# Sharing the first tile's high parts, squaring four chunks at a time, and moving the last square: a hybrid decoder layer on one core

## The chip, the cores and the metric

The kernel runs on one core of a Trainium2 chip. The core has a matrix engine (TensorE, PE in the profile), three engines for element-wise work (VectorE or DVE, ScalarE or ACT, GpSimd or POOL) and queues for transfers (the one on SyncE is SP). Each engine works through its own list of instructions in order and waits on semaphores for the others. The metric is device time of one execution in microseconds (us), the median over several runs; lower is better.

## The reference

One layer of a decoder trunk, for 1024 positions of width 1024, in float32:

```python
h = rmsnorm(x, norm1_w)
proj = h @ w_in                       # one projection for both mixers
qkv_a = silu(causal_dwconv(...))      # mixer A: gated DeltaNet, 4 heads of 128
o_a = gated_delta_rule(l2norm(qa) * 128 ** -0.5, l2norm(ka), va, g, beta)
o_a = rmsnorm(o_a, gdn_norm_w) * silu(z)
o_b = dilated_attention(qb, kb, vb)   # mixer B: 8 heads of 64, three windows
x = x + concatenate([o_a, o_b]) @ w_out
h = rmsnorm(x, norm2_w)
u = causal_dwconv(h @ w_up, ffn_conv_w)
x = x + (silu(gate) * up) @ w_down    # gate and up are the halves of u
return rmsnorm(x, final_norm_w)
```

`rmsnorm` divides by the root of the mean square over the features. In the gated delta rule every head carries a 128x128 state through the sequence, chunk by chunk, and `o_a` is normalized per position and head.

## The kernel before, in words

Activations are held with features on the 128 partitions and positions along the row, so `x` is eight tiles (`xt`) of 128x1024. Every large float32 product is done as three products of a faster type: each operand is split into a high part and the low rest (`xhi`, `xlo`, `whi`, `wlo`), and `mm3` adds hi*hi, hi*lo and lo*hi. Below, a product of 128x512 of this kind is called a dense product.

**The order of the work.** A planner (`Weave`) runs the parts of the layer as generators ("streams") with levels of urgency. It keeps an estimate of when each tile will be ready (`account`, with a fixed cost and a cost per element for each engine, by the size of the first tile named in the call) and steps the most urgent stream that is ready. The order in which it records the products is PE's order. The instructions of the other engines are put in order by a scheduler behind it, by their priority and its own estimates; `ua` and `uv` are ScalarE and VectorE with high priority, `ac` and `ve` the same engines without, and `after` makes one instruction stand behind another on its engine.

**The parts that the change touches.**

- *The first tiles.* Nine warm-up products (`warm`) run while the first transfers land. `split_x` makes the high part of a tile of `x` on ScalarE (scaled by `n1`, the weights of the first norm) and then the low part on VectorE. Tile 0 comes in two halves of 512 positions; PE begins when the first half's high part is there. `first` does the first six banks of products (keys of three heads); beside it `norms` sums the squares (`acc`) on PE with a vector `ones`, makes `rst` (one over the root) and transposes it into `rstdB`, and `gates` makes the decays. `kprep` then works on a head's keys `kT`: it turns them by token (`ktok`), squares them and multiplies keys by keys (PE `ps<-kT`).
- *The chains.* `chain(h)` carries the state of one head through eight chunks of 128 positions. A step is a string of small products and short operations that need each other: `ct,kT` on PE, `r` on VectorE, `r,um` on PE, `wke` on VectorE and `w` on ScalarE, `wke,ktok` on PE, and the new state `ct` on VectorE. The output of chunk c lands in `vtok`; its square with the sum over the row (`osq`, `ms`) is taken on ScalarE. After the last chunk the whole head is scaled by a power of `ms` on GpSimd, and `finish` transposes it. Four chains run interleaved with dense products, which fill the waits of one chain.
- *The end.* The last stage of the MLP's down-projection (`mlp_down`) treats the last four output tiles by halves of 256 positions. `last_product` adds a bank to the residual (`add_to`), and `complete` squares the result for the final norm. The last square (`apart`) isn't added to the others but summed on PE as a second operand (`more` in `mean_of`). Then come the power on GpSimd, two transposes (`turned`), eight scalings (`scale_out`) and the last transfers. Scalings of tiles that are ready earlier are put behind the addition of the last bank by `anchor=fourth`.

Of the kernel before, what the change touches and what calls it, by code (L numbers as in the profile page):

```python
# [7 lines left out]
F32 = mybir.dt.float32  # L8
F32R = mybir.dt.float32r
AF = mybir.ActivationFunctionType  # L10
OP = mybir.AluOpType
AX = mybir.AxisListType
# [3 lines left out]
P = 128  # L16
# [131 lines left out]
def hybrid_layer(tc, I, out):  # L148
    nc = tc.nc
    wv = Weave()  # L150
    ve = Engine(wv, nc.vector, "vector", 0.07, 0.00105)
    ac = Engine(wv, nc.scalar, "scalar", 0.12, 0.00085)

    uv = Engine(wv, nc.vector, "vector", 0.07, 0.00105, first=tc.high_priority)
    ua = Engine(wv, nc.scalar, "scalar", 0.12, 0.00085, first=tc.high_priority)
# [7 lines left out]
    sp = es.enter_context(tc.tile_pool(name="sp", bufs=1))  # L163
# [3 lines left out]
    def tile_(pool, shape, dt, name, tag, bufs):  # L167
        return wv.slot(pool.tile(list(shape), dt, name=name, tag=tag, bufs=bufs), tag, bufs)
# [3 lines left out]
    def A(name, tag, dt=F32, shape=(P, 1024)):  # L172
        if tag in TURNS:
            i = turns[tag] = turns.get(tag, -1) + 1
            tag = TURNS[tag][i % len(TURNS[tag])]
        return tile_(lp, shape, dt, name, tag, SLOTS[tag])
# [4 lines left out]
    def const(name, shape, src=None):  # L181
        t = cp.tile(list(shape), F32, name=name)
        if src is not None:
            sy.dma_start(t, src)
        return t
# [3 lines left out]
    def after(inst, anchor, reason="keeps a slot free until it is needed"):  # L189
        tc.add_manual_dep(inst.ins, anchor.ins.name, order, reason=reason)  # L190

    def mm(dst, lhs, rhs, us, start=True, stop=True, **kw):
        tc.stamp_issue_order_token(nc.tensor.matmul(dst, lhs, rhs, start=start, stop=stop, **kw).ins, TOKEN)  # L193
        wv.product(us, dst, lhs, rhs)
# [47 lines left out]
    n1 = const("n1", [P, KT])  # L242
# [6 lines left out]
    def rsqrt(dst, src, n):  # L249
        po_.tensor_tensor(dst, src, mhalf[:, :n], op=OP.pow)  # L250
# [14 lines left out]
    def bank(tag, name="ps"):  # L265
        return tile_(pp_, (P, 512), F32, name, tag, 2)

    def next_bank(tag, *tiles, slack=0.0):

        while max(wv.need(*tiles), wv.slot_free(tag, 2)) + slack > 1e-3:  # L270
            yield max(wv.need(*tiles), wv.slot_free(tag, 2)) + slack
        return bank(tag)

    def half(i):
        return slice(i * 512, i * 512 + 512)

    def v8(t):
        return t.rearrange("p (c t) -> p c t", c=NCH)
# [7 lines left out]

    def split_x(xt, k, sl):
        hi, lo = xs[k]
        inst = ua.activation(hi[:, sl], xt[:, sl], AF.Copy, scale=n1[:, k:k + 1])
        if k == 0:  # L290
            after(inst, his[0] if sl.start else whis[0], "in the order of arrival")
        if k == 1:
            after(inst, whis[1], "the weights come first")
        his[k:] = [inst]
        lo_of[0] = uv.scalar_tensor_tensor(lo[:, sl], xt[:, sl], n1[:, k:k + 1], hi[:, sl].bitcast(F32), op0=OP.mult,
                                           op1=OP.subtract)
# [19 lines left out]
    for k in range(KT):  # L316
        xt = A("xt", ("kT*", "dv*")[k % 2])
# [200 lines left out]
    def small(name, bufs=2):  # L518
        return tile_(sp, (P, NCH), F32, name, name, bufs)
# [316 lines left out]
    def chain_load(h, s):  # L836
        t = A("qat", "go" if s == 1 and h < 2 else "qa", shape=(P, 2, 512))
        sy.dma_start(t[:, 0, :], qpark[h][:, half(s)])
        sy.dma_start(t[:, 1, :], atpark[h][:, half(s)])
        return t  # L840
# [3 lines left out]
    def chain(h):  # L844

        for i in range(H):
            yield from wv.until(("m", i))
            yield from wv.until(("v", i))
        d = G[h]
        kT, ktok, vtok, yt, ge, rq, gq, ke = [d[n] for n in ("kT", "ktok", "vtok", "yt", "ge", "rq", "gq", "ke")]  # L850
        if not ct:
            ct.append(A("ct", "uy", shape=(P, 8, P)))
        sts = ct[0][:, 2 * h:2 * h + 2, :]
        qa = chain_load(h, 0)
        ps = bank(("asc", "ch")[h // 2])
        ms = small("ms", 4)
        tg = str(h)
        st = None
        for c in range(NCH):
            cs = slice(c * P, (c + 1) * P)  # L860
            if c == 2 and h < 2:
                qb = chain_load(h, 1)
            if c == 3 and h >= 2:
                yield from wv.until(("c", h - 2, 3))
                qb = chain_load(h, 1)
            if c == 4:
                qa = qb
            qT, at = [qa[:, i, (c % 4) * P:(c % 4 + 1) * P] for i in range(2)]
            if c == 0:
                r = vtok[:, cs]  # L870
                yield wv.need(ps, vtok, yt)
            else:
                yield wv.need(ps, st, slack=HOP)
                mm(ps[:, 0:P], kT[:, cs], st, 0.215)
                r = tile_(sp, [P, P], F32, "r", "r" + tg, 1)
                uv.scalar_tensor_tensor(r, ps[:, 0:P], ngam[:, c, h:h + 1], vtok[:, cs], op0=OP.mult, op1=OP.add)
                yield wv.need(r, slack=HOP)
            mm(ps[:, P:2 * P], yt[:, c, :], r, 0.215)
            w = tile_(sp, [P, P], F32, "w", "w" + tg, 1)
            if c < NCH - 1:  # L880
                wke = tile_(sp, [P, P], F32, "wke", "r" + tg, 1)
                uv.tensor_scalar(wke, ps[:, P:2 * P], ke[:, c:c + 1], None, op0=OP.mult)
            ua.activation(w, ps[:, P:2 * P], AF.Copy)
            if c < NCH - 1:
                yield wv.need(wke, slack=HOP)
                mm(ps[:, 2 * P:3 * P], ktok[:, cs], wke, 0.215)
                sn = sts[:, c % 2, :]
                if c == 0:
                    uv.tensor_copy(sn, ps[:, 2 * P:3 * P])
                else:  # L890
                    uv.scalar_tensor_tensor(sn, st, ge[:, c:c + 1], ps[:, 2 * P:3 * P], op0=OP.mult, op1=OP.add)
            yield wv.need(w, qa, slack=HOP)
            po = yield from next_bank("atr")
            if c:
                mm(po[:, P:2 * P], qT, st, 0.215)
            mm(po[:, :P], at, w, 0.215)

            ua.activation(vtok[:, cs], po[:, :P], AF.Copy, scale=rq[:, c:c + 1])
            if c:
                uv.scalar_tensor_tensor(vtok[:, cs], po[:, P:2 * P], gq[:, c:c + 1], vtok[:, cs], op0=OP.mult,  # L900
                                        op1=OP.add)
            if c < NCH - 1:
                st = sn
            osq = tile_(sp, [P, P], F32, "osq", "osq", 1)
            ua.activation(osq, vtok[:, cs], AF.Square, accum_out=ms[:, c:c + 1])
            wv.done.add(("c", h, c))

        ve.tensor_scalar(ms, ms, 1.0 / 128, EPS, op0=OP.mult, op1=OP.add)
        rsqrt(ms, ms, NCH)
        po_.tensor_tensor(v8(vtok), v8(vtok), ms[:, :, None].to_broadcast([P, NCH, P]), op=OP.mult)  # L910
        wv.add(1, finish(h, vtok))

    def finish(h, osb):
        for hh in range(2):
            pt = yield from next_bank("atr", osb)
            for c in range(4):
                i = 4 * hh + c
                tp(pt[:, c * P:(c + 1) * P], osb[:, i * P:(i + 1) * P])
            ot = tile_(sp, [P, 512], F32, "ot", "t2", 2)
            ac.activation(ot, pt, AF.Copy, scale=gw2)  # L920
            sy.dma_start(mixer[h][:, half(hh)], ot)
        wv.done.add(("o", h))
# [589 lines left out]
    def part(m, hh, sl):  # L1512
        return slice(512 * hh + sl.start, 512 * hh + sl.stop)
# [6 lines left out]
    def complete(m, hh, sl, apart=False):  # L1520

        sp_ = part(m, hh, sl)
        x = x1h[m][:, sp_]
        sq = tile_(sp, [P, 512], F32, "sq3", "t2", 2)
        ac.activation(sq[:, sl] if m else rstdB[:, sp_], x, AF.Square)
        if apart:
            return sq
        if m:
            ve.tensor_tensor(rstdB[:, sp_], rstdB[:, sp_], sq[:, sl], op=OP.add)

# [93 lines left out]
    for h in range(H):  # L1624
        wv.add(1, chain(h))
# [65 lines left out]
```

## Time and the profile before

| | us |
|---|---|
| median of 3 runs | 1201.8 |
| the three runs | 1199.36, 1201.80, 1201.89 |
| the profiled execution: its time | 1200.36 |
| its span in the profile | 1198.6 |
| PE busy in it | 1187.5 |
| VectorE, ScalarE, GpSimd busy | 915.1, 574.8, 89.8 |

The span runs from the first instruction to the last; 1.8 us of the execution's time lie outside it. In rows of the timeline the first two numbers are the start in the span and the duration, then come engine, line, operation and the tiles (written <- read); what stands in brackets is the idle time of that engine just before, and what ended it. Tile names are those of the program, without buffer numbers, and all operations of a helper have its line: L193 is `mm`, L197 `tp`, L142 and L144 the calls of the engines without and with high priority.

### The profile page before, as it was taken

How to read it: one execution, taken by the hardware profiler on the slowest of the kernel's cores; microseconds unless marked ns; L12 is line 12 of the kernel's file. 1: busy time of each engine (PE TensorE's matmuls, PEld its weight loads, DVE VectorE, ACT ScalarE, POOL GpSimd, SP SyncE). 2: the span in 40 equal slices, each digit the busy share in tenths (PEclk: the TensorE clock that was granted, in tenths of full speed). 3: DMA queues.
4: the chain of work that ended last, by engine and by line, in shares of the span. 5: the costliest groups of instructions: out<-in, count | busy, mean ns of one | idle time of the engine just before them, and what ended most of it. 6: DMA issues, size and time to landing. Idle time of an engine off the chain costs nothing.

```text
span 1198.6 us, 18324 instructions
## 1 busy us (share of the span) xinstructions
PE 1187.5 (99%) x7050; PEld 983.7 (82%) x7050; DVE 915.1 (76%) x1450; ACT 574.8 (48%) x1126; POOL 89.8 (7%) x100
## 2 busy tenths in 40 slices
PE   9999999999999999999999999999999999999997
PEld 7888888888777778888888888888888888888886
DVE  7683975665355566777989888989898889999875
ACT  7275345355454443655544544445445454434441
POOL 0212010214311120000000000000000000000000
PEclk9999999999999999999999999999999999999998
DMA  7435234436634204543213223131222398557414
GB/s 237 107 95 150 85 109 127 152 113 183 224 95 124 73 28 128 180 154 110 88 54 104 90 70 106 53 106 60 99 90 69 109 371 292 192 157 229 160 53 141
DMA packets 85798, 154.80 MB, mean 129 GB/s; under 512 B 21168, under 2 KB 36304, under 8 KB 85712
## 3 DMA queue, kind: packets, MB, share of 16 engines
q1 hardware_dynamic: 84848, 152.85, 39.1%
q8 instruction: 55, 0.90, 0.3%
q10 hardware_dynamic: 864, 0.79, 0.2%
q14 instruction: 31, 0.25, 0.1%
HBM read 117.68 MB, written 35.93 MB: 128 GB/s over the span
## 4 chain that ended last, share of the span: by engine, by line
PE 95%; DVE 2%; ACT 2%; issue 1%; DMA 0%; POOL 0%; POOLq 0%; DVEq 0%; SPq 0%; ACTq 0%
PE ps L193 45%; PE pa L193 20%; PE dw L193 17%; PE pc L193 10%; PE ps L197 3%; DVE kT L142 1%; ACT sm L144 0%; DMA xt<-in_xT 0%; DVE x1h L142 0%; ACT whi L142 0%; PE pd L193 0%; DVE zz L142 0%; ACT dec L142 0%; DVE xr L142 0%; DVE rstdB L142 0%
## 5 line engine op out<-in xcount | busy, mean ns | idle before, releaser
L193 PE MATMUL dw<-pr 128*128 128x512 f32 (+1 forms) x984 | 211.3, 376 | 0.0
L193 PEld LDWEIGHTS dw<-pr 128*128 128x128 f32 x984 | 176.7, 188 | 33.6
L193 PE MATMUL ps<-xhi,whi 128*128 128x512 f32 x384 | 157.7, 411 | 0.3 <-ACT xhi L144 0.3
L193 PE MATMUL ps<-xhi,wlo 128*128 128x512 f32 x384 | 150.3, 391 | 0.0
L193 PE MATMUL ps<-xlo,whi 128*128 128x512 f32 x384 | 148.4, 390 | 0.0
L193 PE MATMUL pa<-T,pair 128*128 128x512 f32 x528 | 127.0, 389 | 0.0
L193 PEld LDWEIGHTS pa<-T,pair 128*128 128x128 f32 x528 | 99.0, 188 | 20.6
L193 PEld LDWEIGHTS ps<-xhi,whi 128*128 128x128 f32 x384 | 72.5, 189 | 19.6 <-issue 5.6
L193 PEld LDWEIGHTS ps<-xhi,wlo 128*128 128x128 f32 x384 | 72.4, 188 | 15.7
L193 PEld LDWEIGHTS ps<-xlo,whi 128*128 128x128 f32 x384 | 72.3, 188 | 12.5
L142 ACT ACTIVATE u<-pa 128x512 f32<-128x512 f32 x44 | 26.3, 598 | 107.2 <-PE pa L193 107.2
L142 DVE SCALAR_TENSOR_TENSOR y<-xu,fcw,y 128x1023 f32<-128x1023 f32 (+1 forms) x44 | 56.4, 1281 | 22.1 <-ACT y L142 22.0
L142 ACT ACTIVATE whi<-wst 128x1024 fp32r<-128x1024 f32 x36 | 38.2, 1063 | 65.4 <-PE ps L193 54.3
L193 PE MATMUL pa<-B,A 128*128 128x512 f32 x264 | 63.4, 389 | 0.0
L193 PE MATMUL pa<-T,S 128*128 128x512 f32 x264 | 63.4, 389 | 0.0
L193 PE MATMUL pc<-B,pair 128*128 128x512 f32 x264 | 63.4, 389 | 0.0
L193 PE MATMUL pc<-T,S 128*128 128x512 f32 x264 | 63.4, 389 | 0.0
L142 DVE TENSOR_TENSOR wst<-wst 128x512 f32<-128x512 f32 x88 | 60.5, 688 | 0.9
L193 PE MATMUL ps<-B,pair 128*128 128x512 f32 x252 | 60.5, 389 | 0.0
L142 POOL TENSOR_TENSOR rs<-rs,mhalf 128x2 f32<-128x2 f32 (+2 forms) x4 | 4.7, 1187 | 738.4 <-DVE rs L144 738.4
L142 ACT ACTIVATE pr<-wd 128x1024 fp32r<-128x1024 f32 x33 | 34.9, 1058 | 49.5 <-PE dw L193 37.0
L144 ACT ACTIVATE sm<-sm,mx 128x128 f32<-128x128 f32 (+7 forms) x64 | 35.4, 556 | 48.2 <-DVE mx L144 48.2
(248 smaller groups left out, 2411.1 us busy)
## 6 DMA issues: line engine op xcount, KB each, us to landing
wst<-in_wu SPq DMA_DIRECT2D x44, 512.0 KB, 3.7
wd<-in_wd SPq DMA_DIRECT2D x44, 512.0 KB, 4.5
upark<-y SPq DMA_DIRECT2D x22, 512.0 KB, 3.6
wst<-in_wi SPq DMA_DIRECT2D x21, 512.0 KB, 3.8
r<-upark SPq DMA_DIRECT2D x11, 512.0 KB, 7.5
r<-upark SPq DMA_DIRECT2D x22, 256.0 KB, 7.5
wa<-in_wd SPq DMA_DIRECT2D x22, 256.0 KB, 3.3
wst<-in_wv SPq DMA_DIRECT2D x8, 512.0 KB, 3.7
```

What stands on the lines that cost most here:

```text
L142: return getattr(eng, op)(*a, **kw)
L144: return getattr(eng, op)(*a, **kw)
L193: tc.stamp_issue_order_token(nc.tensor.matmul(dst, lhs, rhs, start=start, stop=stop, **kw).ins, TOKEN)
L197: tc.stamp_issue_order_token(nc.tensor.transpose(dst, src, ident if idt is None else idt).ins, TOKEN)
```

## The change

Three edits. (1) In `split_x`, for tile 0 alone, the second 256 columns of each half's high part are made by VectorE (a multiplication by `n1`) and only the first 256 by ScalarE. (2) In `chain`, a square with its row sum after every chunk is replaced by one 128x512 square after every fourth chunk, without high priority, and a VectorE reduction that sums it into four columns of `ms`; the tile is now of the ring `t2`, which has two buffers and which other parts use too. (3) In `complete`, the last square is a VectorE multiplication instead of a ScalarE square.

```diff
     def split_x(xt, k, sl):
         hi, lo = xs[k]
-        inst = ua.activation(hi[:, sl], xt[:, sl], AF.Copy, scale=n1[:, k:k + 1])
+        if k == 0:
+            mid = sl.start + 256
+            ve.tensor_scalar(hi[:, mid:sl.stop], xt[:, mid:sl.stop], n1[:, k:k + 1], None, op0=OP.mult)
+            inst = ua.activation(hi[:, sl.start:mid], xt[:, sl.start:mid], AF.Copy, scale=n1[:, k:k + 1])
+        else:
+            inst = ua.activation(hi[:, sl], xt[:, sl], AF.Copy, scale=n1[:, k:k + 1])
...
-            osq = tile_(sp, [P, P], F32, "osq", "osq", 1)
-            ua.activation(osq, vtok[:, cs], AF.Square, accum_out=ms[:, c:c + 1])
+            if c % 4 == 3:
+                osq = tile_(sp, [P, 4, P], F32, "osq", "t2", 2)
+                hs = half(c // 4)
+                ac.activation(osq.rearrange("p c d -> p (c d)"), vtok[:, hs], AF.Square)
+                ve.tensor_reduce(out=ms[:, c - 3:c + 1], in_=osq, op=OP.add, axis=AX.X)
...
         sq = tile_(sp, [P, 512], F32, "sq3", "t2", 2)
+        if apart:
+            ve.tensor_tensor(sq[:, sl], x, x, op=OP.mult)
+            return sq
         ac.activation(sq[:, sl] if m else rstdB[:, sp_], x, AF.Square)
-        if apart:
-            return sq
```

Since the planner counts these operations, its order of the products changes too, though the products stay the same. The following is one piece of the difference on PE between the first dense products: `ps<-ones,acc` are the sums of the norm.

```order
 L193 MATMUL ps<-xlo,whi 128x512
 L193 MATMUL ps<-xhi,wlo 128x512
-L193 MATMUL ps<-xhi,whi 128x512
-L193 MATMUL ps<-xlo,whi 128x512
-L193 MATMUL ps<-xhi,wlo 128x512
+L193 MATMUL ps<-ones,acc 128x1 x2
 L193 MATMUL ps<-xhi,whi 128x512
```

The sums now come where three dense products stood: 99 of these stand ahead of the first sum, and 102 did before. The transposes of `rst`, further on, have 120 ahead of them instead of 126. From the turning of the first keys on, after 192 dense products, PE's order is as before until the chains.

On VectorE in the chains, this is the piece around the second half of the steps of heads 0 and 1, before (numbers tell the buffers apart; `ps_2444` and `ps_2434` are the banks of heads 1 and 0, `ct` with `ge_582` is the state of head 1, `wke_2830` belongs to head 0):

```order
L144 SCALAR_TENSOR_TENSOR r_2812<-ps_2454,ngam_246,vtok_2027 128x128
L144 SCALAR_TENSOR_TENSOR ct_2430<-ct_2430,ge_628,ps_2464 128x128
L144 SCALAR_TENSOR_TENSOR ct_2430<-ct_2430,ge_582,ps_2444 128x128
L144 SCALAR_TENSOR_TENSOR vtok_2411<-ps_2816,gq_2325,vtok_2411 128x128
L144 TENSOR_SCALAR wke_2830<-ps_2434,ke_672 128x128
```

And the same place after (the bank numbers are two higher):

```order
L144 SCALAR_TENSOR_TENSOR r_2792<-ps_2456,ngam_248,vtok_2029 128x128
L144 SCALAR_TENSOR_TENSOR ct_2432<-ct_2432,ge_630,ps_2466 128x128
L142 TENSOR_REDUCE ms_2457<-osq_2773 128x4
L144 SCALAR_TENSOR_TENSOR ct_2432<-ct_2432,ge_584,ps_2446 128x128
L144 SCALAR_TENSOR_TENSOR vtok_2413<-ps_2796,gq_2327,vtok_2413 128x128
L144 TENSOR_SCALAR wke_2808<-ps_2436,ke_674 128x128
```

The reduction of head 2's first four chunks now stands between the two states, ahead of `ct` of head 1 and of `wke` of head 0. The other operations keep their order.

On VectorE at the end of the program, before (`x1h<-x1h,dw` is the addition of a last bank, `x1h<-x1h,fw,ps` scalings of the output, `rs` the mean of the last squares):

```order
L142 SCALAR_TENSOR_TENSOR x1h<-x1h,fw,ps 128x256 x2
L142 TENSOR_TENSOR rstdB<-rstdB,sq_10777 128x256
L142 TENSOR_TENSOR x1h<-x1h,dw 128x256
L142 SCALAR_TENSOR_TENSOR x1h<-x1h,fw,ps 128x256 x2
L144 TENSOR_SCALAR rs_10811<-ps 128x2
L142 SCALAR_TENSOR_TENSOR x1h<-x1h,fw,ps 128x256 x8
```

And after:

```order
L142 SCALAR_TENSOR_TENSOR x1h<-x1h,fw,ps 128x256 x2
L142 TENSOR_TENSOR rstdB<-rstdB,sq_10739 128x256
L142 TENSOR_TENSOR x1h<-x1h,dw 128x256
L142 SCALAR_TENSOR_TENSOR x1h<-x1h,fw,ps 128x256 x2
L142 TENSOR_TENSOR sq_10762<-x1h 128x256
L144 TENSOR_SCALAR rs_10773<-ps 128x2
```

The last square, which was at the end of ScalarE's list, now stands on VectorE behind two scalings of the output and ahead of the mean.

## The prediction

> **What bounds the kernel now.** I read the page first (busy time, the chain that ended last, the groups), then PE's own waits, then the timeline at four places: the first product, the first keys, the four chains, the last microseconds.
>
> ```profile
> span 1198.6 us, 18324 instructions
> PE 1187.5 (99%) x7050; PEld 983.7 (82%) x7050; DVE 915.1 (76%) x1450; ACT 574.8 (48%) x1126; POOL 89.8 (7%) x100
> PE 95%; DVE 2%; ACT 2%; issue 1%; DMA 0%; POOL 0%; POOLq 0%; DVEq 0%; SPq 0%; ACTq 0%
> L142 DVE TENSOR_TENSOR wst<-wst 128x512 f32<-128x512 f32 x88 | 60.5, 688 | 0.9
> ```
>
> PE is busy for 1187.5 of 1198.6 us. The change adds and removes no matrix product, so it can act only through the some 11 us in which PE is idle, and through products that run slowly. This is PE's list of waits (engine, tile, line, releaser: total, times, longest):
>
> ```profile
> PE ps L193 <- ACT w L144: 0.5, 1, 0.5
> PE ps L193 <- DVE ct L144: 0.5, 1, 0.5
> PE ps L193 <- ACT xhi L144: 0.3, 1, 0.3
> PE ps L193 <- ACT sq L142: 0.3, 1, 0.3
> PE ps L193 <- ACT sq L144: 0.2, 1, 0.2
> ```
>
> Each of the five is one event, and each lies where the change has a hand: `xhi` at the start, `sq` of L144 at the first keys, `ct` and `w` in the chains, `sq` of L142 at the end. All five together are 1.8 us, 0.15% of the span. That is the size of this case.
>
> **The start: shared high parts.** The timeline around the first product:
>
> ```profile
> 4.47 0.85 PE L193 MATMUL warm<-warm 128*128 128x128 f32 x3
> 4.88 1.33 ACT L144 ACTIVATE xhi<-xt,n 128x512 fp32r<-128x512 f32 x2 [1.17 <-DMA xt<-in_xT]
> 5.64 1.41 DVE L144 SCALAR_TENSOR_TENSOR xlo<-xt,n,xhi 128x512 fp32r<-128x512 f32 x2 [1.34 <-ACT xhi L144]
> 5.66 0.79 PE L193 MATMUL ps<-xhi,whi 128*128 128x512 f32 x1 [0.34 <-ACT xhi L144]
> 6.25 0.63 PE L193 MATMUL ps<-xhi,wlo 128*128 128x512 f32 x1
> 6.67 0.63 PE L193 MATMUL ps<-xhi,whi 128*128 128x512 f32 x1
> 7.10 0.46 PE L193 MATMUL ps<-xhi,wlo 128*128 128x512 f32 x1
> ```
>
> ScalarE makes both 512-wide halves in 1.33 us, so the first takes about 0.66 us and ends at 5.54; PE starts 0.12 us later. Now ScalarE makes 256 columns. Its 128x256 squares at the end take 0.42 us (row below), so its half ends at 4.88 + 0.42 = 5.30. VectorE was idle for 1.34 us before 5.64 and makes the other 256 meanwhile; nearest row for it is again a 128x256 operation, 0.42 us. PE can start at 5.42, 0.24 us sooner; the warm-up products end at 5.32. What this is worth depends on the clock. Products here start 0.42 to 0.43 us apart up to 7.10, and 0.22 apart later (65.40 and 65.62 below). If the fast rate begins at a fixed time, 0.24 us more of slow running does 0.24/0.425 = 0.56 of a product, worth 0.56 x 0.22 = 0.13 us. If it begins after a fixed number of products, the whole 0.24 is gained. The Trainium skill, page "TensorE: Matmul & The Clock Gate", section "Part 1: The HAM clock gate", says that the warm-up budget is a stretch of time and not a number of matmuls: by that rule the gain is 0.13, without it 0.24. One trace can't show which holds. I take **-0.13 us**, with 0 and -0.24 as ends. The second half's high part now waits on VectorE behind `xlo` of the first half, some 6.4 instead of 6.2; nine products stand ahead of its first reader, so that is covered.
>
> **The first keys: an order that shifts.** The planner is told of the earlier start and puts the sums of the norm three dense products sooner on PE, and the first transposes of `rst` six sooner (126 dense products stood ahead of them, now 120). The rows:
>
> ```profile
> 39.39 1.64 POOL L142 TENSOR_TENSOR rst<-rst,mhalf 128x8 f32<-128x8 f32 x1 [33.98 <-DVE rst L142]
> 42.94 0.60 PE L197 MATMUL ps<-ident,rst 128*128 128x128 f32 x4
> 63.52 1.14 ACT L142 ACTIVATE kT<-xr,gcw 128x1024 f32<-128x1024 f32 x1
> 64.56 0.57 ACT L144 ACTIVATE ktok<-ps 128x512 f32<-128x512 f32 x1
> 65.40 0.39 PE L193 MATMUL ps<-wlo,xhi 128*128 128x512 f32 x1
> 65.62 0.39 PE L193 MATMUL ps<-whi,xlo 128*128 128x512 f32 x1
> 66.20 0.60 PE L193 MATMUL ps<-kT 128*128 128x128 f32 x3 [0.19 <-ACT sq L144]
> ```
>
> `rst` is ready at 41.03 and read at 42.94, a slack of 1.9 us. Sums three products (0.7 us) sooner and readers six products (1.3 us) sooner leave 1.3 us, so no new wait. Everything that hangs on the norm (scaling, convolution, key decays) then runs up to 1.3 us sooner against PE, whose products of the keys stay in place. At 66.20 PE is late: from 65.62 to 66.20 is 0.58 us where 0.22 is the step, because ScalarE turned to `ktok` at 64.56, straight behind other work. If that work is over 0.5 us or more sooner, the whole 0.36 goes. I take **-0.35 us**, with 0 as the other end.
>
> **The chains: squares four at a time.** Removed are 32 squares of 128x128 with their accumulator reads; added are eight squares of 128x512 on ScalarE and eight VectorE reductions.
>
> ```profile
> L144 ACT ACTIVATE osq<-vtok x32: 293/310/312, 248.0 to 304.6; 128x128 f32<-128x128 f32 x32
> L144 ACT ACTIVATION_READ_ACCUMULATOR osq<-vtok x32: 185/187/192, 248.3 to 304.8; 128x1 f32 x32
> 254.28 1.08 DVE L142 TENSOR_TENSOR aqkv<-ps,rstdB 128x512 f32<-128x512 f32 x1 [0.24 <-PE ps L193]
> 255.58 0.49 PE L193 MATMUL ps<-ct,kT 128*128 128x128 f32 x2 [0.45 <-DVE ct L144]
> 271.48 0.68 DVE L144 SCALAR_TENSOR_TENSOR ct<-ct,ge,ps 128x128 f32<-128x128 f32 x2
> 272.34 0.72 DVE L144 TENSOR_SCALAR wke<-ps,ke 128x128 f32<-128x128 f32 x2
> 272.48 0.37 ACT L144 ACTIVATE vtok<-ps,rq 128x128 f32<-128x128 f32 x1 [0.53 <-PE ps L193]
> 272.51 0.39 PE L193 MATMUL ps<-ct,kT 128*128 128x128 f32 x2
> 272.75 0.30 ACT L144 ACTIVATE osq<-vtok 128x128 f32<-128x128 f32 x1
> 273.04 0.43 ACT L144 ACTIVATE w<-ps 128x128 f32<-128x128 f32 x2
> 273.36 0.49 PE L193 MATMUL ps<-wke,ktok 128*128 128x128 f32 x2 [0.47 <-ACT w L144]
> ```
>
> ScalarE loses up to 32 x (0.31 + 0.19) = 16 us and gets back 8 x 0.66 (a 128x512 half of the start) = 5.3. PE had waited for those squares at one place only, 273.36: `w` could not start at 272.75 because `osq` stood ahead. Without it `w` starts 0.29 sooner. But at this very place the new order puts a reduction between the two `ct` on VectorE. No row shows a reduction; the nearest is the 128x512 tensor-tensor, 0.69 us (ends 0.34, one chunk's operation, and 1.08, `aqkv`). The second `ct` ran from 271.81 to 272.16, and PE used it at 272.51. Behind a reduction that starts at 271.74 it starts near 272.35, ends near 272.70, and PE's `ct,kT` comes at about 272.78, 0.27 late. `wke` follows two VectorE steps later, near 273.2, and PE's `wke,ktok` near 273.3: where it stood anyway. One wait takes the place of the other: **0 us**. The wait at 255.58 is `aqkv` ahead of `ct`; both stand as before, so it stays. In the new order the first two reductions have three dense products (0.7 us) behind them before their neighbours on VectorE are read, and the last five have dense products around them, so I cost them at nothing; where that cover fails each costs up to 0.6 us (0.69 less the some 0.08 by which the next VectorE operation starts before the end, as the rows of the end show). The last scaling of a head now waits for a reduction before its power on GpSimd; its transposes stand behind that by more than a microsecond in my count. Bounds for the stage: -0.9 (both waits go) and +3.
>
> **The end: last square on VectorE.**
>
> ```profile
> 1188.99 0.42 DVE L142 TENSOR_TENSOR x1h<-x1h,dw 128x256 f32<-128x256 f32 x1
> 1189.33 0.87 DVE L142 SCALAR_TENSOR_TENSOR x1h<-x1h,fw,ps 128x256 f32<-128x256 f32 x2
> 1189.51 0.42 ACT L142 ACTIVATE sq<-x1h 128x256 f32<-128x256 f32 x1 [1.15 <-DVE x1h L142]
> 1189.97 0.61 PE L193 MATMUL ps<-ones,sq 128*128 128x1 f32 x4 [0.29 <-ACT sq L142]
> ```
>
> Here nothing covers: sum, power, transposes, scaling and output all hang on this square. ScalarE started 0.1 us after the addition and PE followed at 1189.97. On VectorE the square could run from 1189.33, but the new order puts it behind the two scalings that only had to follow the addition. They hold VectorE to 1190.12 (the 1189.33 row starts 0.08 us before the end of the one ahead); a 128x256 square of 0.42 us ends at 1190.54, and with 0.1 to 0.16 us of hand-over PE starts near 1190.67. That is **+0.70 us**; were the square ahead of the scalings, it would be 1189.75 and -0.1.
>
> **The sum.** -0.13 - 0.35 + 0 + 0.70 = +0.22 us on the profiled execution's 1200.36 us: 1200.6. The three timed runs have their median at 1201.8 and reach from 1199.36 to 1201.89, so the profiled one lies inside them. On the median the forecast is 1202.0 us.
>
> **The rivals.** *Reductions stop the chains (slower).* Around 255 and 273 us few or no dense products stand between dependent steps, and the row at 255.58 shows what one long VectorE operation does there: 1.08 us of `aqkv`, 0.45 of wait. If five of the eight reductions cost PE their full 0.6 us, the stage gives +3.0 and the time is 1205.0. It decides from four such reductions on (2.4 us); against it speak the dense products around most. Chance 0.20. *ScalarE's freedom pays (faster).* Both chain waits go (0.45 + 0.47), the start gives 0.24, the keys 0.35, and the end gains 0.1 because the scalings are not ready when the square is: -1.6, so 1200.2. The order on VectorE speaks against the last part, `aqkv` against the first. Chance 0.12. *The split does not do what it says:* VectorE's half ends as late as ScalarE's whole did, the start gives 0, and the time is 1202.1. Chance 0.05. The forecast has 0.63.
>
> **The numbers.** A difference of 0.2% (2.4 us) is about what a measurement of this kernel can tell from none. Forecast and split rival (0.68) lie within it, but for 0.03 at each side that the spread of single runs may carry over. The slow rival gives 0.20 to slower; the fast one crosses the bound only with that spread too, 0.09 of its 0.12. Faster 0.12, same 0.65, slower 0.23. The range leaves out some 0.1 at each side: from 1199.2 (fast rival, a low median) to 1204.8 (nearly all of the slow one).
>
> **What would show it.** In the new profile: PE's first product near 5.4 and the fast rate still from about 7.1; no wait of PE at 66; a reduction of about 0.7 us ahead of `ct` and a wait for `ct` where that for `w` was; the last square behind two scalings and its sums 0.7 us later against the last `dw` product. The forecast is wrong if the chains' stretch grows by more than a microsecond, or if the last sums do not move.

## The result and the profile after

The changed kernel takes 1202.97 us (median of 12 runs, 1202.73 to 1205.33), the kernel before 1200.40 us (median of 12 runs, 1199.36 to 1201.89; the first three runs, on which the forecast stood, had been high ones). The ratio is 1.0024, with a 95% interval of 1.0016 to 1.0032. The change makes the kernel 2.6 us slower; the forecast was +0.2 us. The time lies inside the range, but two of the four terms of the sum were wrong, a third can't be seen in the time, and a wait that the prediction had ruled out is the largest part.

The profiled execution of the changed kernel took 1203.51 us. The head of its page, and then the list of PE's waits (engine, tile, line, releaser: total, times, longest), without four waits that are as before (`ones`, `rs`, `sm`, `rstdB`):

```profile
span 1201.7 us, 18306 instructions
PE 1187.2 (99%) x7050; PEld 982.6 (82%) x7050; DVE 919.4 (77%) x1461; ACT 568.3 (47%) x1069; POOL 90.7 (8%) x100
```

```profile
PE ps L197 <- POOL vtok L142: 1.2, 2, 1.0
PE ps L193 <- DVE sq L142: 0.9, 1, 0.9
PE ps L193 <- ACT xhi L144: 0.8, 1, 0.8
PE ps L193 <- ACT sq L144: 0.6, 1, 0.6
PE ps L193 <- DVE acc L142: 0.5, 1, 0.5
PE ps L193 <- DVE ct L144: 0.5, 1, 0.5
PE ps L193 <- ACT w L144: 0.4, 1, 0.4
```

PE is as busy as before (1187.2 against 1187.5 us); ScalarE has lost 6.5 us of work and VectorE gained 4.3, and neither shows in the span. The waits sum to 4.9 us where the five of before made 1.8. That the difference, 3.1 us, equals that of the two spans is tempting, but the traces of the experiments show that the waits for `xhi` and for `sq` of L144 differ as much between executions with the same order of instructions (0.2 to 1.0 us and 0.2 to 1.1 us). Two of the others are surely the change's own: `vtok` on GpSimd, which was no wait before, and `sq` on VectorE at the end.

The start, in the timeline of the changed kernel:

```profile
5.05 0.91 ACT L144 ACTIVATE xhi<-xt,n 128x256 fp32r<-128x256 f32 x2 [0.66 <-DMA xt<-in_xT]
5.61 0.50 PE L193 MATMUL ps<-xhi,whi 128*128 128x512 f32 x1 [0.81 <-ACT xhi L144]
5.95 0.39 PE L193 MATMUL ps<-xhi,wlo 128*128 128x512 f32 x1
6.18 0.39 PE L193 MATMUL ps<-xhi,whi 128*128 128x512 f32 x1
```

The two shares take 0.91 us on ScalarE instead of 1.33, but the transfer landed 0.17 us later than in the profile before, so the first product stands at 5.61 instead of 5.66. And here the products ran at the fast step (0.23 us) from the second on; in the profile before they had been at 0.43 up to 7.10. The first keys:

```profile
58.88 1.88 DVE L142 SCALAR_TENSOR_TENSOR kT<-xr,kT 128x1024 f32<-128x1024 f32 x1 [0.59 <-ACT xr L142]
60.68 0.16 DVE L142 COPY gel<-dec 128x8 f32<-128x8 f32 x1
67.06 1.16 PE L193 MATMUL ps<-kT 128*128 128x128 f32 x8 [0.57 <-ACT sq L144]
```

The wait that should have gone grew from 0.19 to 0.57. The chains' last two heads, on GpSimd, then on PE, with the operations of ScalarE and VectorE that make the last `ms`:

```profile
294.98 1.64 POOL L142 TENSOR_TENSOR ms<-ms,mhalf 128x8 f32<-128x8 f32 x1 [2.11 <-PE ps L193]
296.85 2.39 POOL L142 TENSOR_TENSOR wlo<-wst,whi 128x1024 fp32r<-128x1024 f32 x1 [0.23 <-ACT whi L142]
299.19 1.90 POOL L142 TENSOR_TENSOR vtok<-vtok,ms 128x1024 f32<-128x1024 f32 x1
...
311.80 2.40 POOL L142 TENSOR_TENSOR wlo<-wst,whi 128x1024 fp32r<-128x1024 f32 x1 [2.72 <-ACT whi L142]
314.16 1.64 POOL L142 TENSOR_TENSOR ms<-ms,mhalf 128x8 f32<-128x8 f32 x1
315.87 1.90 POOL L142 TENSOR_TENSOR vtok<-vtok,ms 128x1024 f32<-128x1024 f32 x1
301.15 1.09 PE L197 MATMUL ps<-ident,vtok 128*128 128x128 f32 x8 [0.25 <-POOL vtok L142]
317.82 1.10 PE L197 MATMUL ps<-ident,vtok 128*128 128x128 f32 x8 [0.96 <-POOL vtok L142]
309.49 0.63 ACT L142 ACTIVATE osq<-vtok 128x512 f32<-128x512 f32 x1 [0.42 <-DVE vtok L144]
310.15 0.69 DVE L142 TENSOR_REDUCE ms<-osq 128x4 f32<-128x512 f32 x1 [0.70 <-ACT osq L142]
310.78 1.13 DVE L142 TENSOR_TENSOR aqkv<-ps,rstdB 128x512 f32<-128x512 f32 x1
311.75 0.17 DVE L142 TENSOR_SCALAR ms<-ms 128x8 f32<-128x8 f32 x1
```

A head's scaling is a power (1.64 us) and a multiplication (1.90) on GpSimd. In the kernel before they followed each other for every head; these are its last two:

```profile
293.24 1.64 POOL L142 TENSOR_TENSOR ms<-ms,mhalf 128x8 f32<-128x8 f32 x1 [1.24 <-DVE ms L142]
294.95 1.90 POOL L142 TENSOR_TENSOR vtok<-vtok,ms 128x1024 f32<-128x1024 f32 x1
296.81 2.38 POOL L142 TENSOR_TENSOR wlo<-wst,whi 128x1024 fp32r<-128x1024 f32 x1
...
305.31 1.64 POOL L142 TENSOR_TENSOR ms<-ms,mhalf 128x8 f32<-128x8 f32 x1 [1.22 <-DVE ms L142]
307.02 1.90 POOL L142 TENSOR_TENSOR vtok<-vtok,ms 128x1024 f32<-128x1024 f32 x1
```

There the next `wlo` came at 310.17 only, and PE's transposes of the fourth head at 311.04, 2.1 us after its scaling had ended. Now a dense weight's low part (`wlo`, 2.4 us) stands between them for the third head and ahead of both for the fourth, where `ms` is ready at 311.92 only: square 0.63, reduction 0.69, and then `aqkv`, 1.13 us, ahead of the small scaling of `ms` on VectorE. PE waits for both heads. The end:

```profile
1191.23 0.42 DVE L142 TENSOR_TENSOR x1h<-x1h,dw 128x256 f32<-128x256 f32 x1
1191.57 0.86 DVE L142 SCALAR_TENSOR_TENSOR x1h<-x1h,fw,ps 128x256 f32<-128x256 f32 x2
1192.35 0.42 DVE L142 TENSOR_TENSOR sq<-x1h 128x256 f32<-128x256 f32 x1
1192.82 0.61 PE L193 MATMUL ps<-ones,sq 128*128 128x1 f32 x4 [0.90 <-DVE sq L142]
```

The sums start 1.59 us after the last addition, where it was 1189.97 - 1188.99 = 0.98: 0.61 us later, through the two scalings, as forecast.

### The profile page after: what moved, and what is told of

The parts are those of the page before. It is cut to its first block, busy times and chain, and to the rows that moved or that the text cites. A ratio compares the mean times of both kernels' runs of the same rounds, so it can differ in the third digit from the quotient of the medians.

```text
span 1201.7 us, 18306 instructions
## 1 busy us (share of the span) xinstructions
PE 1187.2 (99%) x7050; PEld 982.6 (82%) x7050; DVE 919.4 (77%) x1461; ACT 568.3 (47%) x1069; POOL 90.7 (8%) x100
## 4 chain that ended last, share of the span: by engine, by line
PE 71%; DVE 1%; issue 1%; ACT 0%; POOL 0%; POOLq 0%; DVEq 0%; ACTq 0%
PE ps L193 23%; PE pa L193 20%; PE dw L193 17%; PE pc L193 10%; PE ps L197 2%; DVE x1h L142 0%; PE pd L193 0%; DVE zz L142 0%; ACT sm L144 0%; DVE rstdB L142 0%; POOL rs L142 0%; DVE pt L144 0%; POOLq L1696 0%; DVE xr L142 0%; DVE sm L144 0%
## 5 line engine op out<-in xcount | busy, mean ns | idle before, releaser
L142 ACT ACTIVATE pr<-r 128x1024 fp32r<-128x1024 f32 (+1 forms) x44 | 36.5, 839 | 47.0 <-PE dw L193 29.8
L193 PEld LDWEIGHTS pa<-B,A 128*128 128x128 f32 x264 | 49.6, 188 | 10.3
```

The costliest lines, as they stand in the source:

```text
L142: return getattr(eng, op)(*a, **kw)
```

## Experiments

Each was timed in five rounds against the kernel before on the same chip (medians of before there: 1200.15, 1200.25 and 1200.24 us for the three groups). One such ratio is uncertain by 0.0009, about 1.1 us, so the smaller terms are read from the traces. For that the table after the third group cuts each execution at the same products. The edits are shown shortened; a remark behind `#` stands for lines that are left out.

### First group: the edits one by one

**First edit alone.**

```diff
-        inst = ua.activation(hi[:, sl], xt[:, sl], ...)
+        if k == 0:   # 256 columns on VectorE, 256 on ScalarE
```

> The kernel before with the first edit alone (high parts of tile 0 shared). Theory A (the planner's shift costs more than the earlier start gives): the first product comes 0.05 to 0.25 us sooner, but the sums of the norm, three dense products earlier in PE's order, wait about 0.5 us for acc, and the first products of keys by keys still wait about 0.6; together +0.2 to +0.9 us against before (ratio 1.0002 to 1.0008). Theory B (the prediction: -0.13 at the start, -0.35 at the first keys): -0.5 us. Theory C: the waits of the changed kernel at 33 and 67 us came from transfers that landed late in that one execution; then they are gone here and the time is within 0.2 us of before.

Measured: 1200.44 us, ratio 1.0007 (0.9998 to 1.0016). The first product came at 5.36, the wait at the first keys was 0.69 us. The interval reaches from -0.2 to +1.9 us, so theory B's -0.5 lies outside it; theories A and C can't be told apart by the time. The wait for `acc` was down to 0.08 us, but late transfers alone don't explain that of the changed kernel. With the sums where they stood before (eight traced executions, those below included) PE never waited for `acc`, which was ready 0.36 to 1.69 us ahead; with the sums three products sooner (five) it waited 0.08, 0, 0.25, 0.29 and 0.50 us. The shift takes the slack, and how late `acc` is differs from execution to execution. The forecast's -0.35 at the keys did not show.

**Second edit alone.**

```diff
-            ua.activation(osq, vtok[:, cs], AF.Square, accum_out=ms[:, c:c + 1])
+            if c % 4 == 3:   # one 128x512 square and a reduction
```

> The kernel before with the second edit alone (squares four chunks at a time). Theory A (GpSimd's order): the power and the scaling of the heads 2 and 3 stand behind a dense weight's 2.4 us low part, PE waits about 1 us at one pair of head transposes and 0.4 at another, and the time grows by 1.2 to 1.8 us. Theory B (the prediction: one wait takes the place of another, transposes covered): within 0.2 us of before. Theory C (the reductions stop the chains): +3 us, and the waits lie at ct, r or wke on VectorE, not at vtok on GpSimd.

Measured: 1202.01 us, ratio 1.0017 (1.0009 to 1.0026). PE's waits in the chains' stretch of the trace are those of the changed kernel's list: 1.2 us in two events for `vtok` on GpSimd, 0.5 for `ct` and 0.4 for `w`. The last two were 0.5 each before. The new wait is for `vtok` alone: theory A, and no sign of theory C.

At the place that the prediction worked out, the reduction stands at 273.18 between the two `ct`, and the next `ct,kT` on PE comes 0.41 us after the product ahead of it where it was 0.23. The wait for `w` did not go with the square of ScalarE: `w` now waits for `wke`, which stands behind the reduction.

```profile
274.73 0.47 ACT L144 ACTIVATE w<-ps 128x128 f32<-128x128 f32 x2 [0.40 <-DVE wke L144]
```

**Third edit alone.**

```diff
-        ac.activation(sq[:, sl] if m else rstdB[:, sp_], x, AF.Square)
         if apart:
+            ve.tensor_tensor(sq[:, sl], x, x, op=OP.mult)
             return sq
```

> The kernel before with the third edit alone (last square on VectorE). Theory A (the square stands behind two scalings on VectorE): the last sums come 0.6 to 0.7 us later after the last addition, and the time grows by the same 0.6 to 0.7 us. Rival: the end hangs on the output transfers, which queue behind the earlier scalings anyway; then it is within 0.2 us of before.

Measured: 1200.95 us, ratio 1.0013 (1.0004 to 1.0022). The sums start 1.59 us after the last addition, 0.61 later than before, and the last stretch in the table below is 100.30 us where it was 99.69: theory A.

**All three edits, last square first.**

```diff
-            ve.tensor_tensor(sq[:, sl], x, x, op=OP.mult)
+            added.append(ve.tensor_tensor(sq[:, sl], x, x, op=OP.mult))
-        scale_out(0, left, pl, range(6, 8), anchor=fourth)
+        scale_out(0, left, pl, range(6, 8), anchor=added[-1])
```

> The changed kernel with all three edits, but the last two scalings of the left half put behind the last square on VectorE instead of behind the addition, so that the square comes first. Theory A (order is the whole cost of the third edit): 0.6 to 0.8 us less than the changed kernel, so about 1.8 us over before, with the sums waiting for sq about 0.1 to 0.2 us. Rival (VectorE's square is slower than ScalarE's or is handed over later): the gain is under 0.3 us.

Measured: 1202.66 us, ratio 1.0023 (1.0013 to 1.0032); only 0.3 us under the changed kernel by the medians. The trace shows the last stretch at 99.53 instead of 100.19, so 0.66 us came back there; its middle stretch was 0.5 us longer, with one pause of PE for VectorE (`x`) at 502 us that no other execution has at that place. So the medians leave it open, and the trace speaks for the theory.

### Second group: what in each edit costs

**Squares four at a time for the first four chunks only.**

```diff
+            if c == 3:   # as in the change, for chunks 0 to 3
+            if c > 3:    # as before, one square with a row sum
```

> The kernel before with the second edit for the first four chunks only: chunks 4 to 7 keep their square with a row sum on ScalarE, so that ms is ready as early as before, and GpSimd's order is the order of before. Theory A (the cost of the second edit is the late ms and what GpSimd does meanwhile): no wait of PE for vtok, and within 0.3 us of before, 1.4 us under the second edit alone. Rival (the four-chunk squares and reductions cost by themselves, or the three dense products that the planner moves do): half of the 1.4 us or more stays.

Measured: 1200.58 us, ratio 1.0006 (0.9997 to 1.0014). No wait for `vtok`; 1.4 us under the second edit alone by the medians. In the trace the chains' stretch is 164.42 us, 0.4 over before: most of the cost went, not all. PE's list for that stretch has `ct` (0.5 us) and `w` (0.3) and no new wait, so what the rest hangs on stays open.

**Second edit with GpSimd's order mended.**

```diff
-            po_.tensor_tensor(lo, st, hi.bitcast(F32), op=OP.subtract)
+            inst = po_.tensor_tensor(lo, st, hi.bitcast(F32), op=OP.subtract)
+            if "scaled" in last:      # a head's multiplication by ms
+                after(inst, last["scaled"], "the heads go first")
```

> The second edit alone, and in addition each dense weight's low part on GpSimd put behind the last head's scaling that was recorded ahead of it. Nothing else moves: the orders on TensorE, VectorE and ScalarE are those of the second edit alone; on GpSimd two low parts of 2.4 us go behind the scalings of heads 2 and 3. Theory A (GpSimd's order is the cost, not the lateness of ms by itself): the two waits for vtok (1.2 us together, 1.5 us with the hand-over) go, and the time is 1.2 to 1.6 us under the second edit alone, within 0.4 us of before. Rival 1 (ms is late in any case): the longer wait stays at 0.5 us or more. Rival 2 (the dense products then wait for their late low part): a new wait for wlo of about 1 us.

Measured: 1200.40 us, ratio 1.0000 (0.9991 to 1.0009). GpSimd at the last two heads, and PE at the last:

```profile
293.24 1.64 POOL L142 TENSOR_TENSOR ms<-ms,mhalf 128x8 f32<-128x8 f32 x1 [2.12 <-ACT ot L142]
294.95 1.90 POOL L142 TENSOR_TENSOR vtok<-vtok,ms 128x1024 f32<-128x1024 f32 x1
296.81 2.39 POOL L142 TENSOR_TENSOR wlo<-wst,whi 128x1024 fp32r<-128x1024 f32 x1
...
310.92 1.64 POOL L142 TENSOR_TENSOR ms<-ms,mhalf 128x8 f32<-128x8 f32 x1 [4.07 <-DVE ms L142]
312.63 1.90 POOL L142 TENSOR_TENSOR vtok<-vtok,ms 128x1024 f32<-128x1024 f32 x1
314.49 2.40 POOL L142 TENSOR_TENSOR wlo<-wst,whi 128x1024 fp32r<-128x1024 f32 x1
314.59 1.09 PE L197 MATMUL ps<-ident,vtok 128*128 128x128 f32 x8
```

Nothing but GpSimd's order differs from the second edit alone, and the whole cost is gone: 1.6 us by the medians (of two chips), 1.5 in the chains' stretch of the trace. No product waits for its later low part. Theory A, and it prices the rest of the second edit: eight reductions of 0.69 us and eight squares cost nothing that the chains' stretch as a whole shows (163.91 us; before, 164.02). Rival 1 lives on in small: the fourth head's scaling ends at 314.53 and PE reads at 314.59. Counted from the same product (the 5500th from the end, in the table below), its power starts 6.6 us later than before and PE's transposes 4.5 us later, so the late `ms` alone uses up the 2.1 us that were to spare.

**Third edit alone, square first.** The edit is that of the first group's last kernel, on the kernel before.

```diff
+            added.append(ve.tensor_tensor(sq[:, sl], x, x, op=OP.mult))
```

> The kernel before with the third edit alone, the square put ahead of the last two scalings on VectorE. Theory (only the order cost anything): the last sums come 0.1 to 0.2 us sooner than before; the time is 0.7 to 0.9 us under the third edit alone and within 0.2 us of before, too little for a verdict against before. Rival: VectorE's square is later in any case, +0.3 us or more.

Measured: 1200.44 us, ratio 1.0002 (0.9993 to 1.0011). VectorE and PE at the end:

```profile
1188.77 0.42 DVE L142 TENSOR_TENSOR x1h<-x1h,dw 128x256 f32<-128x256 f32 x1
1189.23 0.42 DVE L142 TENSOR_TENSOR sq<-x1h 128x256 f32<-128x256 f32 x1
1189.57 0.86 DVE L142 SCALAR_TENSOR_TENSOR x1h<-x1h,fw,ps 128x256 f32<-128x256 f32 x2
1189.70 0.61 PE L193 MATMUL ps<-ones,sq 128*128 128x1 f32 x4 [0.24 <-DVE sq L142]
```

The sums start 0.93 us after the addition (before 0.98, with the edit as it was 1.59). The order is the whole cost of the third edit. On VectorE the square starts 0.04 us after its own addition ends (1189.19), on ScalarE it was 0.10 (1189.51 after 1189.41); moving it gains 0.05 us.

**First edit, the planner's account unchanged.**

```diff
+            wv.account("scalar", 0.12 + 0.00085 * 512, [hi[:, sl]], [xt[:, sl], n1[:, k:k + 1]], 0.28)
+            nc.vector.tensor_scalar(hi[:, mid:sl.stop], ...)
+                inst = nc.scalar.activation(hi[:, sl.start:mid], ...)
```

> The kernel before with the first edit alone, but the planner's account kept as it was for the whole square of ScalarE, so that the order of the products on TensorE is that of before; only the two engines' shares are new. Theory A (an earlier first product is worth nothing that lasts, since TensorE's slow products end at a time that differs from execution to execution by more than the gain, and the first keys hang on VectorE's gel): the sixtieth product anywhere from 15.4 to 16.1 us as in the runs of an undivided start, and the time within 0.3 us of before. Rival (the gain was real and the moved products gave it back): 0.3 to 0.5 us under before, and the first keys' wait is shorter than in the runs of before's start.

Measured: 1200.09 us, ratio 0.9999 (0.9990 to 1.0008). First product at 5.49, sixtieth at 15.73 us, and a wait of 1.06 us at the first keys, more than five times that of the profile before, with the same order of products. The numbers are those of theory A (what the earlier first product is worth is taken up again behind the table); and the run shows that this wait has two sizes under one order.

### Third group: the two sizes of the first keys' wait, and the mended change

Wherever PE waits there, the first keys start 6.2 us after `gel` ends on VectorE (before: 66.20 and 59.98; changed: 67.06 and 60.84): ScalarE's decays, a weight's high part, `kT`, `ktok` and four squares follow in order. In front of `gel` stands a step of `kT`. Here are this step, `gel` and the keys in the second edit alone, whose order there is that of before; the prediction's rows have the keys of before at 66.20 with a wait of 0.19:

```profile
57.49 2.12 DVE L142 SCALAR_TENSOR_TENSOR kT<-xr,kT 128x1024 f32<-128x1024 f32 x1 [0.59 <-ACT xr L142]
59.54 1.05 DVE L142 COPY gel<-dec 128x8 f32<-128x8 f32 x1
66.82 1.16 PE L193 MATMUL ps<-kT 128*128 128x128 f32 x8 [1.09 <-ACT sq L144]
57.45 1.09 POOL L142 TENSOR_SCALAR_AFFINE_SELECT dec<-dec 128x1024 f32<-128x1024 f32 x1 [0.20 <-ACT xr L142]
```

The same step and the select in the kernel before:

```profile
57.77 1.23 DVE L142 SCALAR_TENSOR_TENSOR kT<-xr,kT 128x1024 f32<-128x1024 f32 x1 [0.59 <-ACT xr L142]
57.88 2.07 POOL L142 TENSOR_SCALAR_AFFINE_SELECT dec<-dec 128x1024 f32<-128x1024 f32 x1 [0.34 <-ACT xr L142]
```

In the first trace the select began 0.04 us ahead of the step, and the step took 2.12 us; in the second the step began 0.11 us ahead of the select and took 1.23, and the select took 2.07 instead of 1.09. Two experiments put that to the test.

**Selects held back, on the kernel before.**

```diff
+        if h:
+            after(inst, first_gel[0], "the first keys' decays go first")
+        if h == 0:
+            first_gel.append(po_.tensor_copy(small("gwait"), gel))
```

> The kernel before, with GpSimd's selects of the decays of heads 1 to 3 held back behind a small copy of head 0's gel; no other order moves. Theory A (VectorE's step ahead of gel runs 1.2 us or some 2.0 us according to whether a select is under way on GpSimd, and the first keys come 6.2 us after gel whatever the start): that step runs about 1.25 us and gel 0.16 us, gel ends some 59.1 if the sixtieth product stands at 16.0, the first keys' wait is 0.2 us or less, and the time is 0.2 to 0.5 us under before, at the edge of what can be told. Rival 1 (the step's length has another cause): it runs 1.9 to 2.1 us again with no select under way. Rival 2 (the later selects hold up the next heads): a new wait of PE near the keys of head 1.

Measured: 1199.63 us, ratio 0.9997 (0.9988 to 1.0005).

```profile
57.40 1.23 DVE L142 SCALAR_TENSOR_TENSOR kT<-xr,kT 128x1024 f32<-128x1024 f32 x1 [0.59 <-ACT xr L142]
58.55 0.17 DVE L142 COPY gel<-dec 128x8 f32<-128x8 f32 x1
59.90 5.14 POOL L142 TENSOR_SCALAR_AFFINE_SELECT dec<-dec 128x1024 f32<-128x1024 f32 x3
65.48 1.05 PE L193 MATMUL ps<-kT 128*128 128x128 f32 x8
```

The step takes 1.23, `gel` 0.17 instead of 1.05, and the keys' wait is gone; no other took its place (two later operations of VectorE now meet the selects, 1.56 and 1.81 us instead of 1.27 and 1.22, and are covered). That is theory A, and the mechanism is shown by the trace; the 0.6 us by which the median lies under before can't be told from nothing.

**All three edits, both orders mended** (the edits of the `wlo` order and of the square together):

```diff
+                after(inst, last["scaled"], "the heads go first")
+        scale_out(0, left, pl, range(6, 8), anchor=added[-1])
```

> All three edits of the change, with the two orders mended: the low parts behind the heads' scalings on GpSimd, and the last square ahead of the two scalings on VectorE. Theory (the whole loss of the change is these two orders; the start is worth nothing): 2.0 to 2.3 us under the changed kernel, so 0.1 to 0.9 us over before; no wait for vtok, and the wait of the first keys about 0.6 us as with the planner's shifted order. Rival (costs add up that single runs did not show): 1 us or more over before.

Measured: 1200.18 us, ratio 0.9998 (0.9989 to 1.0007), 2.8 us under the changed kernel by medians of two chips. That is more than the theory gave, and the 0.1 to 0.9 us over before did not show. The wait at the first keys was 0.57 us. Against the theory, a wait of 0.4 us for `vtok` stayed in this execution: the fourth head's power began at 312.76, released by `ms`, and the scaling ended at 316.37 with PE ready for it at 316.0. So a late `ms` can cost some tenths even with GpSimd's order mended.

**The mended change with the selects held back** (both edits above).

```diff
+            after(inst, first_gel[0], "the first keys' decays go first")
```

> The mended change and the selects held back as well. Theory A: the first keys' wait of about 0.6 us goes too, and the time is 0.3 to 0.6 us under the mended change, between 0.5 us under before and 0.3 over. Rival (in the shifted order the first keys wait because one more step of VectorE stands ahead of gel, whatever GpSimd does): 0.3 us or more of the wait stays.

Measured: 1199.59 us, ratio 0.9993 (0.9984 to 1.0002). No wait at the first keys (they stand at 66.19) and none for `vtok`: theory A. It is the lowest median of all kernels here and surely beats the changed kernel; against the kernel before, the interval still holds no change.

The table gives the start of PE's 5500th product from the end (in the stretch before the chains), and from there the time to the 4000th from the end (behind the chains), to the 500th, and to the last. All traces hold 7050 records of products, and these three are of the same form in each. The first column is the start of record 60 on PE, counted from 0, so that the 18 of the warm-up are 0 to 17; the text calls it the sixtieth product. The last stretch has two sizes under one order, 99.58 and 99.69, by whether the last two transposes stand 0.16 or 0.27 us apart.

| kernel | 60th | 5500th from the end | chains | middle | end | wait at the first keys |
|---|---|---|---|---|---|---|
| before | 16.06 | 231.30 | 164.02 | 696.94 | 99.69 | 0.19 |
| first edit | 15.47 | 231.51 | 163.90 | 696.99 | 99.58 | 0.69 |
| second edit | 15.77 | 231.90 | 165.38 | 697.04 | 99.68 | 1.09 |
| third edit | 15.50 | 231.45 | 163.92 | 697.02 | 100.30 | 0.97 |
| all, square first | 15.77 | 231.39 | 165.38 | 697.53 | 99.53 | 0.59 |
| first four chunks only | 15.70 | 231.42 | 164.42 | 696.95 | 99.58 | 0.21 |
| second edit, GpSimd mended | 15.08 | 230.35 | 163.91 | 697.25 | 99.58 | 0.20 |
| third edit, square first | 15.88 | 231.12 | 163.91 | 697.02 | 99.53 | 0.19 |
| first edit, quiet planner | 15.73 | 231.87 | 163.95 | 697.56 | 99.57 | 1.06 |
| selects held back | 15.69 | 230.62 | 163.89 | 697.03 | 99.68 | 0 |
| all, mended | 15.60 | 231.70 | 164.39 | 696.96 | 99.53 | 0.57 |
| all, mended, selects held back | 15.80 | 231.28 | 163.83 | 696.99 | 99.53 | 0 |
| changed | 15.74 | 232.10 | 165.41 | 696.99 | 100.19 | 0.57 |

## Why the prediction was right or wrong

*The start, -0.13: the gain is there, but can't be seen in the time.* From ScalarE's start on the first tile to the first product it is 0.77 or 0.78 us in the seven traced executions where ScalarE alone makes the high parts, and 0.56 us in the six with shares: 0.21 us sooner, of 0.24 forecast (and 0.56 x 0.22 is 0.12, not 0.13). Four of the seven run at the fast step from the second product on without a pause, and their sixtieth product stands 10.43 to 10.45 us behind ScalarE's start; in two such executions with shares it is 10.21 and 10.25, so there the whole gain is kept. But ScalarE's start, which hangs on the first transfer, lies anywhere from 4.65 to 5.59 us, and slow products make the way from the first product to the sixtieth 9.65 to 10.40 us long. So the sixtieth stands at 15.08 to 16.06 us without shares (mean 15.67) and at 15.47 to 15.80 with them (mean 15.69). The step that failed is the choice between a fast rate from a fixed time and one from a fixed number of products. It is neither: with the same warm-up products from 1.10 us on, the products turn fast at about 4.1 us, still within the warm-up, in the changed kernel and in the third edit alone, and only after 7.1 us in the profile before. The Trainium skill, page "TensorE: Matmul & The Clock Gate", section "Part 1: The HAM clock gate", does say that the activity window runs free of the kernel's start and that the count of slow products varies from run to run; the traces agree, and the prediction used only its other sentence, on time against number. One trace can't show such a spread.

*The first keys, -0.35: wrong, and the term was not the change's to give.* The prediction took 0.19 us of wait from one profile and asked what would make it smaller. Under the order of before the same place waited 0.19, 0.19, 0.20, 0.21, 0.97, 1.06 or 1.09 us in seven executions, 0.56 in the mean; under the planner's shifted order 0.57, 0.57, 0.59 or 0.69, 0.61 in the mean. The shift brought a steady middle in place of two extremes, and no gain. The step that failed reads: "Everything that hangs on the norm (scaling, convolution, key decays) then runs up to 1.3 us sooner against PE". On GpSimd it did: counted from the sixtieth product, the power of `rst` ended 0.4 us sooner in the changed kernel than before, and the first select began 0.9 us sooner. But `gel` on VectorE, on which the keys hang, ended 1.2 us later. The selects that came sooner met the last three steps of `kT` ahead of `gel`, which took 2.12, 2.10 and 1.88 us where before one took 2.12 and the others 1.28 and 1.23. The last step began 43.1 us behind the sixtieth product, against 41.7 before; with the selects held back it is 42.1 in the shifted order and 41.7 in that of before, so 1.0 us of the 1.4 came from the selects and 0.4 from the order itself. Under the order of before, the length of the last step is decided by which of VectorE and GpSimd starts first, by 0.04 to 0.24 us. With the selects held back the wait is gone in both orders, and the step of PE to the first key product is 0.23 us instead of 0.58: the size of the term was right, but it takes another edit to get it.

*The chains, 0: wrong; +1.4 us (165.4 against 163.9 in the table).* The place that the prediction worked out came near: the wait for `ct` stays at 0.5 us, the reduction makes PE's next `ct,kT` 0.2 us later (0.27 forecast), but the wait for `w` stays at 0.4 instead of going, so that this place costs 0.2 and not 0; over the whole stretch that doesn't show. The step that failed is the half sentence on GpSimd, "by more than a microsecond in my count". The fourth head's cover was 2.1 us before, and two things eat it. The late `ms` alone leaves 0.06 us of it, as the run with GpSimd's order mended shows. And a later `ms` changes what the scheduler puts in front of the scaling: 2.4 us of `wlo`, twice. GpSimd's rows before and after show both low parts move ahead; the orders shown ahead of the prediction are those of TensorE and VectorE, and it says nothing of GpSimd's. The slow rival (reductions stop the chains, +3) had the direction by luck: its size for the stage is twice the measured one and its mechanism is not what happened, since mending GpSimd's order alone takes the cost away.

*The end, +0.70: right; 0.61 us measured* at the sums, and 0.61 in the last stretch where the last transposes stand alike (100.30 against 99.69), by the mechanism named. Square-first took it back: -0.05 against before, where the estimate for that case was -0.1.

*The sum.* Forecast +0.2; the two terms that the experiments confirm are +1.4 and +0.6, together 2.0, of the 2.6 measured. The rest is inside the uncertainty of the ratio (1.9 to 3.8 us); the three single edits measure +0.3, +1.9 and +0.8. In the two profiles it lies ahead of the chains (232.10 against 231.30), where executions of one order differ by 1.6 us; whether the shifted order costs something there stays open. That the forecast's absolute time, 1202.0, lies so near to 1202.97 is luck: its base was a median of three runs 1.4 us above that of twelve. The fast rival failed with the keys and the end. The rival on the split gave the same 0 for the start that the time shows, but not for its reason: VectorE's share (0.35 us from 5.07) ended before ScalarE's.

## What to carry to other kernels

When a value becomes ready later, look at every queue that the value's consumer shares: a scheduler can put another operation into the gap, and a long one that goes there holds the consumer up by its whole length, however short the first delay was. When an operation moves to another engine, its price is what already stands in that engine's order at that point; ask first whether one more line of ordering removes it, since here two such lines turned +2.6 us into none. A wait of some tenths of a microsecond near the start of a kernel should be read from several executions before a term is built on it.

## What the hardware showed

The products' step falls to its half at a time that differs by 3 us between executions (about 4.1 to 7.1 us after the span's start), with warm-up products that start alike. From the first product to the sixtieth that makes 9.65 to 10.40 us. The first product itself stands at 5.43 to 6.20 us in the seven executions with the start of the kernel before, since the first transfer lands at different times.

VectorE and GpSimd hold each other up by whole instructions: a step of `kT`, whose inputs both lie in SBUF, takes 1.23 us alone and 1.88 to 2.12 when a select started ahead of it (in the second edit alone the select ends at 58.54 and the step 1.07 us later); the select takes 1.09 alone and 1.95 to 2.12 when the step started first; the copy of 128x8, 0.17 alone, took 1.05 to 1.07 beside a select. The multiplication that reads a PSUM bank (`xr`, 0.68 us) showed no such change. The Trainium skill, page "SBUF — State Buffer", section "SBUF: two separate sides", calls the ports that the two share an exclusive lock for a whole instruction, taken by whichever starts first, and counts VectorE operations with two SBUF inputs among those that need it; the rows of the step agree.
